# Attention's scores and value products in plain fp32: no halves, and the value products at two places of 64 columns

## The chip, the cores and the metric

The kernel runs on one core of a Trainium2 chip. The metric is the device time of one execution in microseconds (us); the median of three executions is given. Engines are named as in the profile: PE is TensorE (PEld its weight loads), DVE is VectorE, ACT is ScalarE, POOL is GpSimd, SP is SyncE, which here only issues DMAs.

## The reference

One layer of a hybrid decoder for 1024 prompt tokens and 8 single-token samples. The part that the change touches is the prompt's attention, 8 heads, causal:

```python
s = (jnp.einsum('bqhd,bkhd->bhqk', qn_b, k_nope, preferred_element_type=jnp.float32)
     + jnp.einsum('bqhr,bkr->bhqk', qr_b, krope, preferred_element_type=jnp.float32)) * scale
s = jnp.where(kpos[None, :] <= qpos[:, None], s, -jnp.inf)
p = jax.nn.softmax(s, axis=-1)
return jnp.einsum('bhqk,bkhd->bqhd', p.astype(v.dtype), v)
```

A key has 64 + 32 = 96 features, a value 64. Around it stand two feed-forward blocks of width 2816, an input projection, an mLSTM group, the samples' attention over 64 pages, an output projection, and a per-layer embedding. All data are fp32.

## The kernel before

Activations lie transposed, features on partitions, 1032 tokens (1024 + 8) along the free axis, in three groups of 344. Every large product is computed from halves: an fp32 operand x is split into `hi` (x rounded to the type fp32r, an ACT cast) and `lo` (x - hi, a DVE or POOL subtraction; the helper `split`), and a product is three fp32r matmuls, hi·hi + hi·lo + lo·hi (`mm3`, lines 196 to 198). Small products, such as those of the mLSTM chunks, the norms' sums and the samples' attention, are plain fp32 matmuls; each of these is two instructions on PE in the trace.

The order of PE's and SP's instructions is that in which the code emits them; the tile framework orders DVE, ACT and POOL. The `Emitter` puts slow chains (samples' attention, per-layer embedding projection) step by step between units of tensor work. Large tiles come from one pool of 43 buffers (`big`, helper `B`) that are reused in the order in which they come free.

Prompt attention, as it stands:

- The projections make q, k and v. `q_rope`, `q_nope` and `k_pair` split their results and write both halves to DRAM; `load_head` reads a head's q and k back, 6 DMAs for a head. `v_all` keeps v in SBUF, for each of 8 key blocks a tile of 8 heads x (64 columns of hi, 64 of lo).
- `att_s` takes query blocks of 128 in two halves Q = 0, 1 of a head. For each it makes the scores (up to 512 keys a matmul group, three matmuls of 128 to 512 columns, tile `pss`), the masked maximum (DVE), the exponential with its sum (ACT), the reciprocal and the normalisation (DVE or ACT). Result: P.
- `att_pv` takes the four query blocks of a half together. For each key block kb it transposes the live blocks of P on PE (`pT`), and evacuates them as halves: ACT casts hi, then DVE subtracts lo (tile `PT`). Then two matmuls of up to 512 columns accumulate into `po`, with the stationary operand [v hi | v lo] of 128 columns, so that rows 0 to 63 of `po` collect v hi's part and rows 64 to 127 v lo's. At the end ACT copies one part and DVE adds the other (`aT`).

Transposes run `SKEW` = 3 key blocks ahead of the products, scores 3 blocks of queries ahead (`LEAD`). A head's two halves give 12 key-block steps, 96 steps in all; 48 of them have all four query blocks live (512 columns), 16 each have 3, 2 and 1 (384, 256, 128 columns).

The samples' attention (`sample_attention`, lines 1026 to 1140) runs among this: POOL gathers pages by indirect DMA (`kt`, `nt`, 128 gathers), and PE multiplies them at four places of 32 columns each (`ss`, line 1072; `ol`, line 1118), in plain fp32.

Of the kernel before, what the change touches and what calls it, by code (L numbers as in the profile page):

```python
# [7 lines left out]
F32 = mybir.dt.float32  # L8
F32R = mybir.dt.float32r
# [44 lines left out]
ACT_NORM = (1, 3, 5)  # L54
SKEW = 3
LEAD = 3
AHEAD = 4
# [33 lines left out]
class Emitter:  # L91
    """Orders what is emitted: a step can be put off until some microseconds of tensor work lie before it,
    and slow chains are taken step by step between the units of tensor work."""

# [37 lines left out]
def trunk(ctx: ExitStack, tc, I, O):  # L132
# [73 lines left out]
    class Acts:  # L206
        """Eight feature tiles, split, cut by token group: 15 of a group's 16 slices in five tiles of its own."""

# [74 lines left out]
    class Norm:  # L283
# [137 lines left out]

    # ---- start
    ones = C([128, 128], name="ones")
# [50 lines left out]

    # ---- constants of the mixing part
    ident = C([128, 128], name="ident")
# [28 lines left out]

    # ---- input projection
    zs = {}
# [66 lines left out]
    def gates():  # L574
# [90 lines left out]

    # ---- mLSTM of the prompt, a chunk a step
    xd = tc.dram_tile([MH, 128, NC, CH], F32, name="xd")
# [87 lines left out]

    # ---- norms of the latents
    cks = C([128, 2, NB_S], name="cks")
# [14 lines left out]

    # ---- one step of the mLSTM for the samples, a head at a time
    xs = C([128, MH * NB_S], name="xs")
# [87 lines left out]

    # ---- MLA projections, kept in DRAM until their head's turn
    vd = tc.dram_tile([8, 128, HEADS * 128], F32, name="vtd")
    kd = tc.dram_tile([HEADS * 64, 2, S], F32, name="ktd")
    qnd = tc.dram_tile([HEADS * 64, 2, T], F32, name="qnd")
    qrd = tc.dram_tile([HEADS * 32, 2, T], F32, name="qrd")
    qz = qzr[0:96, :].rearrange("p (a b c) -> p a b c", a=3, b=NB_S)
# [20 lines left out]
    def put_q(dst, rows, qp):  # L889
        def f():  # L890
            for i in range(2):
                sp.dma_start(out=dst[rows, i, :], in_=qp[i].bitcast(F32))
        em.later(6.0, f)

    def q_rope(r, w):
        qp = pair("qr")
        for g in range(G):
            c = GS[g]
            p1, p2 = PS([128, N]), PS([128, N])
            mmk(p1, w[0], cq, c)  # L900
            mmk(p2, w[1], cq, c)
            qf, t2 = SC(p="qf"), SC(p="t2")
            dve.tensor_tensor(out=qf, in0=p1, in1=cos4[:, c], op=ALU.mult)
            dve.tensor_tensor(out=t2, in0=p2, in1=sin4[:, c], op=ALU.mult)
            pool.tensor_tensor(out=qf, in0=qf, in1=t2, op=ALU.add)
            split(qp[0][:, c], qp[1][:, c], qf, pool)
            if g == G - 1:
                for j in range(4):
                    dve.tensor_copy(qz[64:96, 2, :, 4 * r + j], qf[32 * j:32 * j + 32, N - NB_S:N])
            em.spend(2.6)  # L910
        put_q(qrd, slice(128 * r, 128 * r + 128), qp)

    def q_nope(p, w):
        ukT = B([64, 2, 256], F32, "ukT")
        sp.dma_start(out=ukT, in_=I["w_ukT"][:, 2 * p:2 * p + 2, :])
        qp = pair("qn")
        for g in range(G):
            c = GS[g]
            ps = PS([128, N])
            mmk(ps, w, cq, c)  # L920
            split(qp[0][:, c], qp[1][:, c], ps)
            if g == G - 1:
# [31 lines left out]
    def k_pair(p, w):  # L954
        for hf in range(2):
            c = slice(hf * 512, (hf + 1) * 512)
            ps = PS([128, 512])
            mmk(ps, (w[0][:, p], w[1][:, p]), ck, c)
            kk = B([128, 2, 512], F32R, "kk")
            split(kk[:, 0], kk[:, 1], ps)  # L960
            em.later(KD_LAT, lambda c=c, kk=kk: sp.dma_start(out=kd[128 * p:128 * p + 128, :, c], in_=kk.bitcast(F32)))
            em.spend(1.3)

    def v_all(uvh, uvl):
        for kb in range(8):
            ps = PS([128, 512])
            t = slice(kb * 128, (kb + 1) * 128)
            for ct in range(2):
                mm3(ps, ck[ct][0][:, t], ck[ct][1][:, t], uvh[:, ct, :], uvl[:, ct, :], ct == 0, ct == 1)
            vv = B([128, HEADS, 128], F32R, "vv")  # L970
            split(vv[:, :, 0:64], vv[:, :, 64:128], ps.rearrange("p (h v) -> p h v", h=HEADS))
            vtok.append(vv)
            em.spend(1.3)
            yield

    def load_head(hd):
        kp = kT[hd % 2]
        qp = (B([96, S], F32R, "qTh"), B([96, S], F32R, "qTl"))
        for i in range(2):
            sp.dma_start(out=qp[i][0:64, :].bitcast(F32), in_=qnd[64 * hd:64 * hd + 64, i, 0:S])  # L980
            sp.dma_start(out=qp[i][64:96, :].bitcast(F32), in_=qrd[32 * hd:32 * hd + 32, i, 0:S])
            sp.dma_start(out=kp[i][0:64, :].bitcast(F32), in_=kd[64 * hd:64 * hd + 64, i, :])
        return qp
# [15 lines left out]
    for p in range(4):  # L999
        k_pair(p, uk)  # L1000
        if p == KT_AT:
            kT = []
            for i in range(2):
                kp = (B([128, S], F32R, "kTh"), B([128, S], F32R, "kTl"))
                split(kp[0][64:96, :], kp[1][64:96, :], kr[:, 0:S], pool)
                kT.append(kp)
            kr = None
        if p == LH_AT:
            qps = {0: load_head(0)}
# [5 lines left out]

    # ---- attention of the samples over their pages
    NI = NB_S * N_PAGES
# [122 lines left out]

    # ---- attention of the prompt
    em.flush()

    def att_s(hd, qp, Q, P):
        kp = kT[hd % 2]
        for qb in range(4 * Q, 4 * Q + 4):
# [13 lines left out]
            for kg in range(nkg):  # L1160
                n = min(512, nk - 512 * kg)
                ps = PS([128, 512], "pss")
                kc = slice(512 * kg, 512 * kg + n)
                pe.matmul(ps[:, 0:n], qp[0][:, qs], kp[0][0:96, kc], start=True, stop=False)
                pe.matmul(ps[:, 0:n], qp[0][:, qs], kp[1][0:96, kc], start=False, stop=False)
                pe.matmul(ps[:, 0:n], qp[1][:, qs], kp[0][0:96, kc], start=False, stop=True)
                if kg == nkg - 1:
# [19 lines left out]
    def att_pv(hd, P, Q):  # L1187
        po = PS([128, 512], "po")
        nkb = 4 * Q + 4
        pxs = {}  # L1190

        def tr(kb):
            j0 = max(0, kb - 4 * Q)
            ps = PS([128, 4, 128], "pT")
            for j in range(j0, 4):
                pe.transpose(ps[:, j, :], P[j][:, kb * 128:(kb + 1) * 128], ident)
            px = B([128, 2, 4, 128], F32R, "PT")
            split(px[:, 0, j0:4, :], px[:, 1, j0:4, :], ps[:, j0:4, :])
            pxs[kb] = px
# [4 lines left out]
        for kb in range(nkb):  # L1204
# [4 lines left out]
            px = pxs.pop(kb)  # L1209
            for i in range(2):  # L1210
                pe.matmul(po[:, j0 * 128:512], vtok[kb][:, hd, :], px[:, i, j0:4, :].rearrange("p j q -> p (j q)"),  # L1211
                          start=(kb == 0 and i == 0), stop=(kb == nkb - 1 and i == 1))
            px = None
        r0 = 64 * (hd % 2)
        t = aT[hd // 2][r0:r0 + 64, 512 * Q:512 * Q + 512]
        act.copy(t, po[0:64])
        dve.tensor_tensor(out=t, in0=po[64:128], in1=t, op=ALU.add)
        yield
# [56 lines left out]

    # ---- output projection of the mixing part
    n2 = Norm(None, "xn", G_FF2)
# [142 lines left out]

    # ---- per-layer embedding and the final norm
    def ple_unit(m, g):
# [168 lines left out]
```

## Time and profile before

| what | value |
|---|---|
| three executions | 2379.78, 2379.93, 2381.81 us; median 2379.93 |
| span of the profiled execution | 2381.1 us (clock granted on average 0.980) |
| PE busy | 2294.8 us, 96% of the span |
| DVE, ACT, POOL busy | 1084.0, 732.8, 416.5 us |
| chain that ended last | PE 82%, DVE 9%, DMA 4%, ACT 3% |

The profiled execution's time is given by its span alone; it lies between the lowest and the highest of the three, 1.2 us over the median. "Busy" of PE includes the end of each matmul that overlaps the next one's start, so that a busy PE need not be at its peak. Prompt attention lies from 1144 us (first `pss`) to about 1419 us (last `po`) after the start.

### The profile page before, as it was taken

The page shows a single profiled execution, that of the slowest core. Times are in us where ns is not written, and L with a number is a line of the kernel's source. Part 1 is how long each engine was busy: PE and PEld are TensorE (multiplying, and loading weights), DVE is VectorE, ACT ScalarE, POOL GpSimd, SP SyncE. Part 2 cuts the span into 40 slices and gives each one's busy share as a digit, 9 for nine tenths or more (in the row PEclk, how much of TensorE's full clock was granted, in tenths as well). Part 3 has the DMA queues.
Part 4 walks back from the last instruction along what each step waited for, and adds up shares of the span by engine and source line. Part 5 has one row for each costly group of instructions (what it writes and reads, how often), then busy time and mean ns, then how long its engine had stood idle before and what let it go on. Part 6 is the DMA issues. An engine that isn't in the chain of part 4 may idle for free.

```text
span 2381.1 us, 35330 instructions
## 1 busy us (share of the span) xinstructions
PE 2294.8 (96%) x14479; PEld 2220.7 (93%) x14479; DVE 1084.0 (46%) x2231; ACT 732.8 (31%) x1496; POOL 416.5 (17%) x403
## 2 busy tenths in 40 slices
PE   8999999999998999999888889999999999999997
PEld 7999999999998999999666679999999999999996
DVE  7332332333335656447766677623223223223575
ACT  5211211202213334444655553411121120211353
POOL 4101101101103321102565314200000000000233
PEclk9999999999999999999989989999999999999998
DMA  3111011120121313224964530111111112112213
GB/s 134 38 52 60 29 55 54 32 75 28 43 75 59 109 48 93 82 86 165 260 164 134 160 136 28 45 38 52 55 33 54 56 32 70 33 38 78 62 38 107
DMA packets 77883, 177.84 MB, mean 75 GB/s; under 512 B 11200, under 2 KB 37408, under 8 KB 77720
## 3 DMA queue, kind: packets, MB, share of 16 engines
q1 hardware_dynamic: 67432, 153.22, 21.1%
q0 software_dynamic: 6832, 18.12, 2.9%
q10 hardware_dynamic: 3456, 4.23, 0.6%
q8 instruction: 114, 1.87, 0.3%
q14 instruction: 49, 0.40, 0.1%
HBM read 146.58 MB, written 28.95 MB: 74 GB/s over the span
## 4 chain that ended last, share of the span: by engine, by line
PE 82%; DVE 9%; DMA 4%; ACT 3%; issue 2%; POOL 1%; SPq 0%; ACTq 0%; DVEq 0%; POOLq 0%
PE pd L197 7%; PE pd L198 7%; PE pd L196 7%; PE pg L198 7%; PE pu L197 7%; PE pu L196 7%; PE pu L198 7%; PE pg L197 7%; PE pg L196 7%; PE pz L197 3%; PE pz L196 3%; PE pz L198 3%; DVE xf L279 2%; PE po L1211 1%; DMA kt<-in_cT,idx_t 1%
## 5 line engine op out<-in xcount | busy, mean ns | idle before, releaser
L196 PE MATMUL pd<-hdh,wh 128*128 128x344 f32 x1056 | 341.0, 323 | 5.8 <-ACT hdh L178 5.8
L197 PE MATMUL pd<-hdl,wh 128*128 128x344 f32 x1056 | 340.0, 322 | 3.4 <-DVE hdl L182 3.3
L197 PE MATMUL pg<-xn,wh 128*128 128x344 f32 x1056 | 338.6, 321 | 4.5 <-DVE xn L182 3.8
L198 PE MATMUL pd<-hdh,wl 128*128 128x344 f32 x1056 | 339.7, 322 | 0.0
L196 PE MATMUL pg<-xn,wh 128*128 128x344 f32 x1056 | 338.1, 320 | 0.9 <-ACT xn L178 0.9
L196 PE MATMUL pu<-xn,wh 128*128 128x344 f32 x1056 | 338.5, 321 | 0.3 <-DVE si L347 0.3
L198 PE MATMUL pu<-xn,wl 128*128 128x344 f32 x1056 | 337.8, 320 | 0.8 <-DVE wl L182 0.8
L198 PE MATMUL pg<-xn,wl 128*128 128x344 f32 x1056 | 337.9, 320 | 0.5 <-DVE wl L182 0.3
L197 PE MATMUL pu<-xn,wh 128*128 128x344 f32 x1056 | 337.9, 320 | 0.0
L178 ACT CAST wh<-wr 128x1024 fp32r<-128x1024 f32 (+2 forms) x195 | 180.4, 935 | 371.8 <-PE pd L197 291.2
L182 DVE TENSOR_TENSOR wl<-wr,wh 128x1024 fp32r<-128x1024 f32 (+2 forms) x195 | 215.5, 1105 | 116.3 <-ACT wh L178 111.5
L353 DVE TENSOR_TENSOR hp<-si,pu 128x344 f32<-128x344 f32 x132 | 67.7, 513 | 420.5 <-PE pu L198 413.0
L365 DVE SCALAR_TENSOR_TENSOR h<-pd,h 128x344 f32<-128x344 f32 x240 | 123.2, 515 | 280.1 <-PE pd L198 280.1
L254 POOL TENSOR_TENSOR sq<-sq,sq 128x344 f32<-128x344 f32 x66 | 70.6, 1070 | 798.6 <-ACT sq L249 770.7
L196 PEld LDWEIGHTS pd<-hdh,wh 128*128 128x128 f32 x1056 | 200.0, 189 | 7.1 <-ACT hdh L178 6.7
L197 PEld LDWEIGHTS pg<-xn,wh 128*128 128x128 f32 x1056 | 198.7, 188 | 6.4 <-DVE xn L182 5.2
L197 PEld LDWEIGHTS pd<-hdl,wh 128*128 128x128 f32 x1056 | 200.0, 189 | 4.6 <-DVE hdl L182 4.2
L198 PEld LDWEIGHTS pd<-hdh,wl 128*128 128x128 f32 x1056 | 200.0, 189 | 0.0
L196 PEld LDWEIGHTS pg<-xn,wh 128*128 128x128 f32 x1056 | 198.6, 188 | 1.5 <-ACT xn L178 1.2
L198 PEld LDWEIGHTS pg<-xn,wl 128*128 128x128 f32 x1056 | 198.7, 188 | 1.1 <-DVE wl L182 1.1
L198 PEld LDWEIGHTS pu<-xn,wl 128*128 128x128 f32 x1056 | 198.6, 188 | 1.1 <-DVE wl L182 1.1
L196 PEld LDWEIGHTS pu<-xn,wh 128*128 128x128 f32 x1056 | 198.6, 188 | 1.0 <-issue 0.8
(384 smaller groups left out, 4174.9 us busy)
## 6 DMA issues: line engine op xcount, KB each, us to landing
wr<-in_wu SPq DMA_DIRECT2D x44, 512.0 KB, 3.6
wr<-in_wg SPq DMA_DIRECT2D x43, 512.0 KB, 3.7
wr<-in_wd SPq DMA_DIRECT2D x64, 320.0 KB, 2.9
wr<-in_w_in SPq DMA_DIRECT2D x22, 512.0 KB, 3.8
h<-in_xT SPq DMA_DIRECT2D x24, 172.0 KB, 4.2
hsp<-h SPq DMA_DIRECT2D x8, 516.0 KB, 3.4
ppd<-pj SPq DMA_DIRECT2D x24, 172.0 KB, 2.2
h<-hsp SPq DMA_DIRECT2D x8, 516.0 KB, 5.9
```

Of the source, the lines that this page charges most:

```text
L178: act.copy(hi, src)
L182: dve.tensor_tensor(out=lo, in0=src, in1=hi.bitcast(F32), op=ALU.subtract)
L196: pe.matmul(ps, whi, xhi, start=first, stop=False)
L197: pe.matmul(ps, whi, xlo, start=False, stop=False)
L198: pe.matmul(ps, wlo, xhi, start=False, stop=last)
L254: pool.tensor_tensor(out=acc[0], in0=acc[0], in1=q, op=ALU.add)
L279: dve.scalar_tensor_tensor(out=x, in0=s[:, c], scalar=gc[:, g0 + k:g0 + k + 1], in1=r, op0=ALU.mult, op1=ALU.mult)
L353: dve.tensor_tensor(out=p, in0=s, in1=pu, op=ALU.mult)
L365: dve.scalar_tensor_tensor(out=h[m][:, c], in0=pd, scalar=0.5, in1=h[m][:, c], op0=ALU.mult, op1=ALU.add)
L1211: pe.matmul(po[:, j0 * 128:512], vtok[kb][:, hd, :], px[:, i, j0:4, :].rearrange("p j q -> p (j q)"), start=(kb == 0 and i == 0), stop=(kb ...
```

## The change

Scores and value products take fp32 operands as they are. No q, k, v or P is split. A score group is one fp32 matmul instead of three of halves. v is kept as 64 columns a head. In `att_pv` a key block's four transposed query blocks stand in the order 0, 3, 1, 2 (`PV_POS`); the first two are multiplied at columns 0 to 63 of the array, the other two at columns 64 to 127, 256 columns each, with the same v. `PV_LIVE` says which are live on the diagonal. `po` is 256 columns wide, its lower 64 rows holding query blocks 0 and 3, its upper 64 rows 1 and 2. One copy evacuates a transposed block, by DVE for even and by ACT for odd key blocks, and two key blocks share a tile `PT`. Two ACT copies take `po` to `aT`. `load_head` issues 3 DMAs instead of 6; the projections write one DMA where there were two, and `k_pair` one for both halves of the keys.

```diff
     def k_pair(p, w):
-            kk = B([128, 2, 512], F32R, "kk")
-            split(kk[:, 0], kk[:, 1], ps)
-            em.later(KD_LAT, lambda c=c, kk=kk: sp.dma_start(out=kd[128 * p:128 * p + 128, :, c], in_=kk.bitcast(F32)))
+            if hf == 0:
+                kk = B([128, S], F32, "kk")
+            act.copy(kk[:, c], ps)
+            if hf == 1:
+                em.later(KD_LAT, lambda: sp.dma_start(out=kd[128 * p:128 * p + 128, :], in_=kk))
...
     def load_head(hd):
-        qp = (B([96, S], F32R, "qTh"), B([96, S], F32R, "qTl"))
-        for i in range(2):
-            sp.dma_start(out=qp[i][0:64, :].bitcast(F32), in_=qnd[64 * hd:64 * hd + 64, i, 0:S])
-            sp.dma_start(out=qp[i][64:96, :].bitcast(F32), in_=qrd[32 * hd:32 * hd + 32, i, 0:S])
-            sp.dma_start(out=kp[i][0:64, :].bitcast(F32), in_=kd[64 * hd:64 * hd + 64, i, :])
+        qp = B([96, S], F32, "qT")
+        sp.dma_start(out=qp[0:64, :], in_=qnd[64 * hd:64 * hd + 64, :])
+        sp.dma_start(out=kp[0:64, :], in_=kd[64 * hd:64 * hd + 64, :])
+        sp.dma_start(out=qp[64:96, :], in_=qrd[32 * hd:32 * hd + 32, :])
...
     def att_s(hd, qp, Q, P):
-                pe.matmul(ps[:, 0:n], qp[0][:, qs], kp[0][0:96, kc], start=True, stop=False)
-                pe.matmul(ps[:, 0:n], qp[0][:, qs], kp[1][0:96, kc], start=False, stop=False)
-                pe.matmul(ps[:, 0:n], qp[1][:, qs], kp[0][0:96, kc], start=False, stop=True)
+                pe.matmul(ps[:, 0:n], qp[:, qs], kp[0:96, kc], start=True, stop=True)
...
     def att_pv(hd, P, Q):
-        po = PS([128, 512], "po")
+        po = PS([128, 256], "po")
...
-                pe.transpose(ps[:, j, :], P[j][:, kb * 128:(kb + 1) * 128], ident)
-            px = B([128, 2, 4, 128], F32R, "PT")
-            split(px[:, 0, j0:4, :], px[:, 1, j0:4, :], ps[:, j0:4, :])
+                pe.transpose(ps[:, PV_POS[j], :], P[j][:, kb * 128:(kb + 1) * 128], ident)
+            if kb % 2 == 0:
+                pts[:] = [B([128, 2, 4, 128], F32, "PT")]
+            px = pts[0][:, kb % 2]
+            live = (slice(0, 4), slice(1, 4), slice(1, 4, 2), slice(1, 2))[j0]
+            if kb % 2 == 0:
+                dve.tensor_copy(px[:, live, :], ps[:, live, :])
+            else:
+                act.copy(px[:, live, :], ps[:, live, :])
...
-            for i in range(2):
-                pe.matmul(po[:, j0 * 128:512], vtok[kb][:, hd, :], px[:, i, j0:4, :].rearrange("p j q -> p (j q)"),
-                          start=(kb == 0 and i == 0), stop=(kb == nkb - 1 and i == 1))
+            v = vtok[kb][:, 64 * hd:64 * hd + 64]
+            for i, p0 in enumerate(PV_LIVE[j0]):
+                if p0 < 2:
+                    pe.matmul(po[64 * i:64 * i + 64, p0 * 128:256], v, px[:, 2 * i + p0:2 * i + 2, :].rearrange("p j q -> p (j q)"),
+                              start=kb == 0, stop=kb == nkb - 1 - i)
```

`q_rope`, `q_nope` and `v_all` lose their `split` in the same way (one ACT or DVE copy, or none).

On PE, where the second half of head 0 is multiplied with v (`pss` scores of a later block, `ss` the samples' pages, `pT` transposes of P, `po` the value products), there stood before:

```order
L1164 MATMUL pss_11144<-kTh_10529,qTh_10754 128x512
L1165 MATMUL pss_11144<-kTl_10530,qTh_10754 128x512
L1166 MATMUL pss_11144<-kTh_10529,qTl_10755 128x512
L1164 MATMUL pss_11149<-kTh_10529,qTh_10754 128x256
L1165 MATMUL pss_11149<-kTl_10530,qTh_10754 128x256
L1166 MATMUL pss_11149<-kTh_10529,qTl_10755 128x256
L1211 MATMUL po_10989<-PT_11057,vv_10696 128x512 x2
L1196 MATMUL pT_11163<-ident,P_10876 128x128
L1211 MATMUL po_10989<-PT_11095,vv_10729 128x512 x2
L1211 MATMUL po_10989<-PT_11104,vv_10751 128x384 x2
```

and now, at the same place:

```order
L1166 MATMUL pss_11005<-kT_10479,qT_10671 128x512
L1166 MATMUL pss_11008<-kT_10479,qT_10671 128x256
L1221 MATMUL po_10870<-PT_10925,vv_10603 64x256 x2
L1198 MATMUL pT_11020<-ident,P_10773 128x128
L1221 MATMUL po_10870<-PT_10960,vv_10651 64x256 x2
L1221 MATMUL po_10870<-PT_10960,vv_10651 64x128
L1221 MATMUL po_10870<-PT_10960,vv_10651 64x256
```

Nothing has moved past anything else on PE: the same steps follow each other, with fewer and different matmuls in them. Over the kernel the value products stand in 75 unbroken runs, before as now, with transposes, scores or other products of the full array between them.

On SP, where head 1 is loaded (`qnd`, `qrd`, `ktd` are the DRAM copies of q's two parts and of k; `nk` belongs to the samples, `out_n_s` is an output), there stood before:

```order
L980 DMA qTh_10754<-qnd 64x1024
L981 DMA qTh_10754<-qrd 32x1024
L982 DMA kTh_10529<-ktd 64x1024
L980 DMA qTl_10755<-qnd 64x1024
L981 DMA qTl_10755<-qrd 32x1024
L982 DMA kTl_10530<-ktd 64x1024
L1030 DMA nk<-cks 96x8
```

and now:

```order
L814 DMA out_n_s<-nst 128x32
L982 DMA qT_10671<-qnd 64x1024
L983 DMA kT_10479<-ktd 64x1024
L984 DMA qT_10671<-qrd 32x1024
L1032 DMA nk<-cks 96x8
```

Three transfers of a head's six are gone, for each of the 8 heads; SP's whole queue is 34 transfers shorter.

## Rows read from the trace of the kernel before

**Rows 1.** The page's 40 slices of the span, 59.5 us each, in tenths:

```profile
PE   8999999999998999999888889999999999999997
PEclk9999999999999999999989989999999999999998
```

**Rows 2.** Busy time by stretch: length, engines' busy us (instructions), granted clock, DMA share, GB/s:

```profile
1060.00:1144.00 84.00, 80.08 (x498) 74.61 (x497) 58.50 (x173) 42.65 (x98) 22.38 (x17) 0.96 0.55 182
...
1165.00:1200.00 35.00, 30.94 (x186) 20.21 (x186) 19.65 (x60) 18.35 (x48) 26.46 (x28) 0.76 0.83 212
1200.00:1250.00 50.00, 40.94 (x280) 31.59 (x279) 35.42 (x105) 29.14 (x79) 31.81 (x34) 0.91 0.64 169
1250.00:1300.00 50.00, 45.77 (x306) 35.40 (x304) 34.61 (x112) 30.74 (x86) 22.66 (x25) 0.98 0.46 128
1300.00:1350.00 50.00, 41.02 (x267) 31.78 (x268) 28.80 (x86) 25.52 (x68) 29.37 (x32) 0.84 0.60 161
1350.00:1419.00 69.00, 57.58 (x340) 49.05 (x339) 53.72 (x136) 46.31 (x112) 8.20 (x7) 0.90 0.42 147
```

**Rows 3.** Waits of PE, 1140 to 1420 us: total us, times, longest:

```profile
PE ss L1072 <- DMA kt<-in_cT,idx_t: 7.0, 7, 2.8
PE ol L1118 <- DMA nt<-in_cN,idx_n: 6.3, 3, 2.5
PE po L1211 <- DVE PT L182: 6.1, 11, 1.1
PE pT L1196 <- DVE PT L182: 5.9, 1, 5.9
```

**Rows 4.** Timeline of PE, fp32r scores of 512 and of 128 columns:

```profile
1229.83 0.39 PE L1165 MATMUL pss<-kTl,qTh 96*128 96x512 f32 x1
1230.06 0.40 PE L1166 MATMUL pss<-kTh,qTl 96*128 96x512 f32 x1
...
1230.90 0.28 PE L1165 MATMUL pss<-kTl,qTh 96*128 96x128 f32 x1
1231.02 0.28 PE L1166 MATMUL pss<-kTh,qTl 96*128 96x128 f32 x1
```

**Rows 5.** Timeline of PE, plain fp32 products on the full array, two instructions each:

```profile
979.81 0.39 PE L708 MATMUL pc<-vt,kw 128*128 128x129 f32 x2
980.04 0.39 PE L711 MATMUL pab<-vt,w 128*128 128x129 f32 x2
...
2289.17 0.74 PE L263 MATMUL ns<-sq,ones 128*128 128x344 f32 x2
...
2289.91 0.32 PE L197 MATMUL pl<-xp,wh 128*128 128x344 f32 x1
2290.07 0.32 PE L198 MATMUL pl<-xp,wl 128*128 128x344 f32 x1
```

**Rows 6.** Timeline of PE around a samples' block at four places of 32 columns:

```profile
1274.17 0.60 PE L1196 MATMUL pT<-ident,P 128*128 128x128 f32 x4
1274.70 1.50 PE L1072 MATMUL ss<-kt,qz 96*32 96x256 f32 x24
1276.13 0.50 PE L1164 MATMUL pss<-kTh,qTh 96*128 96x512 f32 x1
1276.46 0.39 PE L1165 MATMUL pss<-kTl,qTh 96*128 96x512 f32 x1
```

**Rows 7.** Groups by line: evacuations; busy us, mean ns, idle before:

```profile
L182 DVE TENSOR_TENSOR PT<-pT,PT 128x512 fp32r<-128x512 f32 (+1 forms) x96 | 50.3, 549 | 6.2 <-ACT PT L178 5.6
L178 ACT CAST PT<-pT 128x512 fp32r<-128x512 f32 (+1 forms) x96 | 43.3, 489 | 12.4 <-PE pT L1196 12.2
L1217 DVE TENSOR_TENSOR aT<-po,aT 64x512 f32<-64x512 f32 x16 | 11.1, 694 | 1.0 <-ACT aT L1216 0.2
L544 DVE COPY z<-pz 128x344 f32<-128x344 f32 x15 | 7.3, 496 | 4.5 <-PE pz L198 4.5
```

**Rows 8.** Waits of POOL, 1140 to 1420 us: total us, times, longest:

```profile
POOL nt L1058 <- PE po L1211: 17.7, 5, 9.0
```

More of the change, by code (lines that the diff above doesn't have):

```diff
@@ L55 @@
 SKEW = 3
+PV_POS = (0, 2, 3, 1)
+PV_LIVE = ((0, 0), (1, 0), (1, 1), (1, 2))
 LEAD = 3
@@ L864, in trunk @@
     vd = tc.dram_tile([8, 128, HEADS * 128], F32, name="vtd")
-    kd = tc.dram_tile([HEADS * 64, 2, S], F32, name="ktd")
-    qnd = tc.dram_tile([HEADS * 64, 2, T], F32, name="qnd")
-    qrd = tc.dram_tile([HEADS * 32, 2, T], F32, name="qrd")
+    kd = tc.dram_tile([HEADS * 64, S], F32, name="ktd")
+    qnd = tc.dram_tile([HEADS * 64, S], F32, name="qnd")
+    qrd = tc.dram_tile([HEADS * 32, S], F32, name="qrd")
     qz = qzr[0:96, :].rearrange("p (a b c) -> p a b c", a=3, b=NB_S)
@@ L890, in f @@
         def f():
-            for i in range(2):
-                sp.dma_start(out=dst[rows, i, :], in_=qp[i].bitcast(F32))
+            sp.dma_start(out=dst[rows, :], in_=qp[:, 0:S])
         em.later(6.0, f)
     def q_rope(r, w):
-        qp = pair("qr")
+        qp = B([128, T], F32, "qr")
         for g in range(G):
@@ L901, in q_rope @@
             mmk(p2, w[1], cq, c)
-            qf, t2 = SC(p="qf"), SC(p="t2")
+            qf, t2 = qp[:, c], SC(p="t2")
             dve.tensor_tensor(out=qf, in0=p1, in1=cos4[:, c], op=ALU.mult)
@@ L905, in q_rope @@
             pool.tensor_tensor(out=qf, in0=qf, in1=t2, op=ALU.add)
-            split(qp[0][:, c], qp[1][:, c], qf, pool)
             if g == G - 1:
@@ L915, in q_nope @@
         sp.dma_start(out=ukT, in_=I["w_ukT"][:, 2 * p:2 * p + 2, :])
-        qp = pair("qn")
+        qp = B([128, T], F32, "qn")
         for g in range(G):
@@ L920, in q_nope @@
             mmk(ps, w, cq, c)
-            split(qp[0][:, c], qp[1][:, c], ps)
+            act.copy(qp[:, c], ps)
             if g == G - 1:
@@ L969, in v_all @@
                 mm3(ps, ck[ct][0][:, t], ck[ct][1][:, t], uvh[:, ct, :], uvl[:, ct, :], ct == 0, ct == 1)
-            vv = B([128, HEADS, 128], F32R, "vv")
-            split(vv[:, :, 0:64], vv[:, :, 64:128], ps.rearrange("p (h v) -> p h v", h=HEADS))
-            vtok.append(vv)
+            if kb % 2 == 0:
+                vv = B([128, 2, HEADS * 64], F32, "vv")
+            dve.tensor_copy(vv[:, kb % 2], ps)
+            vtok.append(vv[:, kb % 2])
             em.spend(1.3)
@@ L1003, in trunk @@
             for i in range(2):
-                kp = (B([128, S], F32R, "kTh"), B([128, S], F32R, "kTl"))
-                split(kp[0][64:96, :], kp[1][64:96, :], kr[:, 0:S], pool)
+                kp = B([128, S], F32, "kT")
+                pool.tensor_copy(kp[64:96, :], kr[:, 0:S])
                 kT.append(kp)
@@ L1187, in att_pv @@
     def att_pv(hd, P, Q):
-        po = PS([128, 512], "po")
+        po = PS([128, 256], "po")
         nkb = 4 * Q + 4
         pxs = {}
+        pts = []
         def tr(kb):
@@ L1195, in tr @@
             for j in range(j0, 4):
-                pe.transpose(ps[:, j, :], P[j][:, kb * 128:(kb + 1) * 128], ident)
-            px = B([128, 2, 4, 128], F32R, "PT")
-            split(px[:, 0, j0:4, :], px[:, 1, j0:4, :], ps[:, j0:4, :])
+                pe.transpose(ps[:, PV_POS[j], :], P[j][:, kb * 128:(kb + 1) * 128], ident)
[3 more added lines that the diff above has]
+            live = (slice(0, 4), slice(1, 4), slice(1, 4, 2), slice(1, 2))[j0]
+            if kb % 2 == 0:
+                dve.tensor_copy(px[:, live, :], ps[:, live, :])
+            else:
+                act.copy(px[:, live, :], ps[:, live, :])
             pxs[kb] = px
@@ L1209, in att_pv @@
             px = pxs.pop(kb)
-            for i in range(2):
-                pe.matmul(po[:, j0 * 128:512], vtok[kb][:, hd, :], px[:, i, j0:4, :].rearrange("p j q -> p (j q)"),
-                          start=(kb == 0 and i == 0), stop=(kb == nkb - 1 and i == 1))
+            v = vtok[kb][:, 64 * hd:64 * hd + 64]
[3 more added lines that the diff above has]
+                              start=kb == 0, stop=kb == nkb - 1 - i)
             px = None
         r0 = 64 * (hd % 2)
-        t = aT[hd // 2][r0:r0 + 64, 512 * Q:512 * Q + 512]
-        act.copy(t, po[0:64])
-        dve.tensor_tensor(out=t, in0=po[64:128], in1=t, op=ALU.add)
+        t = aT[hd // 2][r0:r0 + 64, 512 * Q:512 * Q + 512].rearrange("p (j q) -> p j q", j=4)
+        act.copy(t[:, 0:4:3, :], po[0:64].rearrange("p (j q) -> p j q", j=2))
+        act.copy(t[:, 1:3, :], po[64:128].rearrange("p (j q) -> p j q", j=2))
+        pts.clear()
         yield
```

## The prediction

> **What bounds the kernel now.** I read the slices first. PE stands at 9 tenths nearly everywhere, and at 8 in five slices in a row, the twentieth to the twenty-fourth, which are 1131 to 1428 us, the stretch of attention; in two of them the granted clock shows 8 tenths as well [rows 1]. The stage before, where q, k and v are made, has PE busy 80.08 of 84 us [rows 2]: whatever DVE and ACT lose there by no longer splitting hides behind PE and is worth at most those 4 idle us, 1 by my choice. So the change is decided between 1144 and 1419 us.
>
> In that stretch no single engine is the bound. Between 1165 and 1419 us PE is idle 4.1 + 9.1 + 4.2 + 9.0 + 11.4 = 38 us, while DVE is busy 54 to 78% of each window [rows 2]. The clock is granted at 0.76 to 0.98 of full speed; as it knows only 1.2 and 2.4 GHz, a mean c over a window means (1 - c)/0.5 of it at the lower one: 16.8 + 9 + 2 + 16 + 13.8 = 58 us [rows 2]. Work done there takes twice as long, so this costs up to 29 us; PE is idle for part of it, and I take 24. What PE waits for is of two kinds: the samples' gathered pages, 7.0 + 6.3 us, and the evacuation of transposed P, 6.1 + 5.9 us [rows 3]. The clock is lowest in the two windows that hold gathers (0.76 and 0.84) and nearly full in 1250 to 1300, which has few [rows 2].
>
> **Scores: +10 us.** A 512-column fp32r matmul takes 0.23 us from start to start, 0.455 ns a column; one of 128 columns 0.12 [rows 4]. Three of them: 0.70 us at 512, 0.525 at 384, 0.35 at 256, 0.35 at 128. Plain fp32 is two instructions: 0.23 us for 129 columns; and a pair of 344 columns, with one fp32r matmul of 0.16 behind it, takes 0.74, so 0.58 alone [rows 5]. Both give 1.7 ns a column: 0.87 us at 512, 0.65 at 384, 0.435 at 256, 0.22 at 128. There are 48 score groups of 512 and 16 of each other size: 48 x 0.17 + 16 x (0.125 + 0.085 - 0.13) = 8.2 + 1.3, some 10 us of PE work more. DVE and ACT wait 0.17 us longer for a full group.
>
> **Value products: 0 if the two places run side by side.** A full step was two fp32r matmuls of 512 columns, 0.47 us. It becomes two fp32 matmuls of 256 columns, 0.435 us each. No row shows two places of 64. The nearest is the samples' block at four places of 32: 24 instructions of 256 columns, 12 matmuls, in 1.43 us [rows 6], where one after another 12 x 0.435 = 5.2 us would be needed; four abreast 1.31. So I take side by side: 48 full steps save 1.5 us; the 16 steps with three live blocks (0.435 for 0.35) give 1.4 back, the others change by nothing. The other bound is one after another: 48 x 0.40 + 16 x (0.305 + 0.20) = +27 us.
>
> The Trainium skill's "TensorE: Matmul & The Clock Gate" (Part 3) measured only 2.38x for three matmuls side by side in columns. By that share of the ideal two places would give 1.59x, a full step 0.55 us and the value products +6 us in all; the samples' block shows the fuller overlap, 3.6x of 4, drains included.
>
> **Changes of the array's shape: +20 us.** This is the price that the diff does not show. Before the samples' block the fourth transpose starts at about 1274.50 (three steps of 0.11 from 1274.17) and should be done at 1274.61; the block starts at 1274.70, 0.09 late. It takes 0.12 over 1.31. The score matmul behind it takes 0.33 to the next start, where 0.23 is usual: 0.10 [rows 4, 6]. In all 0.31 us for going into the split array and out again. Value products stand in 75 runs with full-array work on both sides, so 75 x 0.31 = 23 us; with 64 columns to load in place of 32, perhaps 25. Some runs wait for their `PT` anyway (11 waits in [rows 3]) and drain meanwhile: I take 20. Bounds: 10, if PE's idle time swallows half of it, and 25.
>
> "TensorEngine Tiling (Array Packing)" in the Trainium skill says under Key Properties that changing the tiling mode drains the engine. This is the rule that speaks against the change; it gives no price, and without it the sum would be 20 us lower.
>
> **Evacuation: -9 us.** DVE loses 96 subtractions (50.3 us) and 16 additions (11.1). It gets 48 copies; one of 344 columns takes 0.50 us [rows 7], so with 512 about 0.67 and over the mix of sizes about 0.55: 26 us. DVE does 35 us less. ACT loses 96 casts of 0.49 (43.3 us) for 48 copies like them, 23 us, and has 32 copies to `aT` where it had 16. The chain from a transpose to its product is one operation of 0.5 to 0.7 us where it was two [rows 7]. PE's 12 us of waits for `PT` [rows 3] should fall to about 4, and waits for softmax by 1.
>
> **Gathers: -11 us.** Tiles of P, q, k and v go from two halves to one: 8 tiles of v become 4, a head's q and k 2 instead of 4, `PT` one for two steps. The 43 buffers are reused in the order of release, so each gather gets a buffer that has been free for longer; POOL waited 17.7 us for PE to release them [rows 8]. SP's queue has 34 transfers fewer ahead of the page table and the loads. I let PE's 13.3 us of waits for pages [rows 3] fall to 3, and add 1 for k's first load. If POOL's own pace sets the pages' arrival, this gain is 4; then PE is held up later by the same pages.
>
> **Clock: -11 us.** Where those stalls go, part of the 58 us at 1.2 GHz should go: I take 11 of the 24 us that they cost. Bounds: 0, and 18.
>
> **The rest: -5 us.** 30 us of new PE work stretch the stage for DVE, ACT and POOL, which have less to do. Of the 38 - 13 - 12 = 13 idle us that are left, I let 5 be filled. With 1 for the projections the sum is 10 + 0 + 20 - 9 - 11 - 11 - 5 - 1 = -7 us.
>
> The sum is against the profiled execution, whose span of 2381.1 us is 1.2 over the median, so the median should move from 2379.9 to 2373. 0.2% of it, 4.8 us, is about what a measurement here can tell from no change.
>
> **Rivals.**
> - *The gains and the prices cancel.* For it: +30 of new PE work is counted from rows, -37 is waits and clock, counted by choice. If the clock follows only half as well (-5) the sum is -1. Time 2376 to 2384. Chance 0.20.
> - *The shape changes make PE the bound: slower.* The 75 drains stand in PE's own queue, and nothing behind them can start. If all are paid (25 us), and POOL's pace keeps the pages late (gain 4) and with them the clock (-5), the sum is 10 + 25 - 9 - 4 - 5 - 5 - 1 = +11 us: 2391. It decides as soon as gathers and clock together give back less than 10. For it: POOL is busy 26.46 of 35 us where the first gathers run [rows 2]. Against it: POOL's wait for buffers [rows 8] is longer than PE's wait for pages. Chance 0.18.
> - *The two places do not run side by side*, so the change does not do what it says: +27 on PE, of which the remaining idle time takes 5 or so, -7 + 22: 2395, up to 2402 with full drains. Against it: the four places [rows 6]. Chance 0.10.
> - *By the 1.59x of above* the time would be 2379, inside the first rival; the trace bears it out so poorly that it adds nothing to its chance.
>
> **How the numbers follow.** The forecast has a chance of 0.52, with its own range from 2353 (clock -18, half of the drains hidden, gathers all gone) to 2375. Faster by over 0.2%: 0.52; within: 0.20; slower: 0.18 + 0.10 = 0.28. The range takes in the first two rivals and most of the third: 2352 to 2401.
>
> **What would show it.** `pss` of 512 columns: two instructions, 0.87 us from the first to the next work. `po`: instructions at both places starting within some hundredths of a us; if the second starts 0.4 us after the first, the third rival is right. Runs of `po` followed by a late first weight load, about 0.3 us a run. PE's waits for `PT` under 5 us, for `kt` and `nt` together under 5, and a granted clock over 0.92 in 1165 to 1419. The forecast is wrong if the clock stays at 0.9 or below although the page waits are gone, if the split array is itself given a lower clock, or if a run costs clearly more than 0.31 us.

## The result, and the profile after

The changed kernel takes 2342.53 us (median of 4 runs, 2340.30 to 2347.29) beside 2379.86 for the kernel before on the same chip: ratio 0.9843, 95% interval 0.9829 to 0.9858, or 37 us less. The forecast was 2373 us, with a range from 2352 to 2401; the time lies below it. The direction was right, the size was not.

The 40 slices of the changed kernel's page, to be read beside [rows 1]; the five slices with an 8 and the two with a low clock are gone:

```profile
PE   8999999999999899999999999999999999999997
PEclk9999999999999999999999999999999999999998
```

Its windows over the same kind of stretches as [rows 2] (length, busy us of PE, PEld, DVE, ACT and POOL with their instructions, granted clock, DMA share, GB/s):

```profile
1060.00:1139.00 79.00, 77.26 (x505) 72.69 (x504) 51.54 (x165) 39.64 (x92) 14.56 (x11) 1.00 0.45 148
1139.00:1200.00 61.00, 56.06 (x349) 33.80 (x348) 42.62 (x146) 35.25 (x93) 45.82 (x49) 0.94 0.72 188
1200.00:1260.00 60.00, 60.00 (x404) 37.08 (x404) 36.85 (x120) 35.48 (x99) 38.40 (x41) 1.00 0.57 158
1260.00:1320.00 60.00, 60.00 (x441) 34.99 (x438) 38.46 (x121) 35.66 (x101) 39.06 (x40) 1.00 0.53 143
1320.00:1380.00 60.00, 56.11 (x348) 37.51 (x345) 42.56 (x109) 39.53 (x94) 7.92 (x7) 0.94 0.53 179
```

From 1200 to 1320 us PE has no idle time at all and the full clock. What it still waits for, 1135 to 1425 us (total us, times, longest), beside [rows 3]: pages 1.9 us where they were 13.3, `PT` 2.4 + 1.5 where it was 12.0:

```profile
PE pT L1198 <- ACT PT L1206: 2.4, 1, 2.4
PE ss L1074 <- DMA kt<-in_cT,idx_t: 1.9, 1, 1.9
PE wom L200 <- DVE wl L184: 1.7, 1, 1.7
PE pj L198 <- ACT wj L180: 1.6, 1, 1.6
PE pj L200 <- DVE wj L184: 1.5, 1, 1.5
PE po L1221 <- DVE PT L1204: 1.5, 1, 1.5
```

The new operations in PE's timeline: score groups of 512 columns, value products of one step (x4: two places, two instructions each) between single transposes, and of two steps (x8):

```profile
1208.89 0.65 PE L1221 MATMUL po<-PT,vv 128*64 128x256 f32 x4
1209.47 0.33 PE L1198 MATMUL pT<-ident,P 128*128 128x128 f32 x1
1209.73 0.65 PE L1221 MATMUL po<-PT,vv 128*64 128x256 f32 x4
...
1216.76 1.88 PE L1166 MATMUL pss<-kT,qT 96*128 96x512 f32 x4
1218.47 0.71 PE L1198 MATMUL pT<-ident,P 128*128 128x128 f32 x5
...
1265.39 1.08 PE L1221 MATMUL po<-PT,vv 128*64 128x256 f32 x8
1266.40 1.77 PE L1166 MATMUL pss<-kT,qT 96*128 96x512 f32 x4
```

Two score groups take 1.71 us from start to start, 0.855 each. One step of value products takes 0.58 to the next start, two take 1.01, so a step is worth 0.43: the two places run side by side. From one run (value products with no other matmul between them) to the next with one transpose between is 0.84 us, where 0.43 + 0.11 would do without a change of shape: 0.30 for out and in.

To see where the 37 us are, one window over the whole attention stage, from the first `pss` to the first `woa`, is best. First the kernel before, then the changed one:

```profile
1144.60:1412.60 268.00, 227.72 (x1419) 175.68 (x1418) 183.11 (x557) 161.86 (x416) 128.03 (x133) 0.89 0.59 162
```

```profile
1139.40:1372.20 232.80, 223.97 (x1484) 135.62 (x1483) 155.44 (x484) 140.72 (x375) 129.59 (x133) 0.97 0.59 167
```

The stage is 35.2 us shorter and starts 5.2 us earlier. I split its length into PE's idle time, what the lower clock costs (as in the prediction: (1 - c)/0.5 of the window, half of it, times PE's busy share) and the rest, PE's work at full clock. Before: 40.3 idle, 0.11/0.5 x 268 = 59 us at 1.2 GHz costing 59/2 x 0.85 = 25, work 202.6. After: 8.8 idle, 14 us at 1.2 GHz costing 6.7, work 217.3. So idle -31.5, clock -18.4, work +14.7.

What the +14.7 is made of can be counted in the traces: the time from the start of one PE instruction to the start of the next, idle time left out and stretches at 1.2 GHz halved. Scores, transposes and value products together take 129.9 us before and 147.1 after, +17.2, with all changes of shape in it. The samples' blocks (`ss`, `ol`) take 27.7 before and 22.1 after, -5.6, though their instructions are the same. What else stands in the stage adds 3.

The two profiled executions are further apart than the medians: their spans are 2381.1 and 2338.5 us, 42.6 apart, beside 37.3. In all other runs the time of an execution is 1.7 to 2.1 us over its span; by that, an estimate, the profiled execution of the kernel before took some 2383 us, 3 over its median and not the 1.2 that the prediction took, and that of the changed kernel, 2340.3, lies 2.2 under its own. Some 5 us of the split are scatter of this kind.

### The profile page after: what moved, and what is told of

Read it like the earlier page. It is cut to its first block, busy times and chain, and to the rows that moved or that the text cites. A ratio compares the mean times of both kernels' runs of the same rounds, so it can differ in the third digit from the quotient of the medians.

```text
span 2338.5 us, 35223 instructions
## 1 busy us (share of the span) xinstructions
PE 2288.4 (98%) x14543; PEld 2178.7 (93%) x14543; DVE 1046.3 (45%) x2147; ACT 708.7 (30%) x1448; POOL 410.4 (18%) x397
## 4 chain that ended last, share of the span: by engine, by line
PE 89%; DVE 6%; ACT 2%; DMA 1%; issue 1%; POOL 0%; SPq 0%; DVEq 0%; ACTq 0%; POOLq 0%
PE pd L199 7%; PE pd L200 7%; PE pd L198 7%; PE pg L200 7%; PE pu L199 7%; PE pu L198 7%; PE pu L200 7%; PE pg L199 7%; PE pg L198 7%; PE pz L199 3%; PE pz L198 3%; PE pz L200 3%; PE pss L1166 3%; DVE xf L281 2%; PE po L1221 2%; PE pT L1198 2%
## 5 line engine op out<-in xcount | busy, mean ns | idle before, releaser
L198 PEld LDWEIGHTS pu<-xn,wh 128*128 128x128 f32 x1056 | 199.0, 188 | 1.0 <-issue 0.8
L199 PEld LDWEIGHTS pu<-xn,wh 128*128 128x128 f32 x1056 | 199.0, 188 | 0.2
```

What stands on the lines that cost most here:

```text
L198: pe.matmul(ps, whi, xhi, start=first, stop=False)
L199: pe.matmul(ps, whi, xlo, start=False, stop=False)
```

## The experiments

Chips are numbered in the order of the experiments. On the first and the fifth the kernel before takes 2378 and 2380 us, as it does beside the result above, on the second to fourth 2422, 2427 and 2427 (last section), so times are compared with neighbours on one chip. On the first and the fifth chip the changed kernel was not run beside the others; its 2342.5 us from the result stands in for it, and the kernels before there lie within 1.5 us of the one beside that result. On the fourth it was not run either. Theory A: room, that is tiles and loads freed, brings the pages in time. Theory B: the shorter evacuation of transposed P. Theory C: longer PE work is taken by idle time.

**Scores alone, value products alone (first chip).**

```
e1: + q, k, att_s of the changed kernel;  v_all, att_pv as before
e2: + v_all, att_pv of the changed kernel;  q, k, att_s as before
```

> Only q, k and the scores go to plain fp32; v, transposed P and the value products stay split as before. Theory A (room: tiles released earlier let the samples' gathers start earlier): 4 of the some 10 big tiles in hand during attention are freed and a head's loads halve, against 10 us more of score work on PE: 2360 to 2375 us, page waits well under the 13 us of before, waits for PT as before (12 us). Theory B (the shorter evacuation of transposed P and the relief of DVE carry the gain): nothing of that is in here, so 2380 to 2390 us, the scores' price alone. Theory C (slower scores give DVE and ACT time, so that the longer PE work itself fills the idle time): 2365 to 2380, with PE's idle time down by 10 and page waits as before.

> Only v, transposed P and the value products go to plain fp32 at two places; q, k and the scores stay split. Theory A: 6 of the some 10 tiles are freed, the shape changes cost their 20 us: 2360 to 2372 us, page waits down to under 5 us. Theory B: the whole gain and none of the scores' price: 2330 to 2342 us, waits for PT near 0 while page waits may stay. Theory C: 2375 to 2395, the shape changes without the cover of slower scores.

Measured: 2354.8 and 2363.5 beside 2378.4 us, ratios 0.9898 (0.9881 to 0.9914) and 0.9936 (0.9920 to 0.9953): -24 and -15 us, which add up to the whole, 37, or a little more. B is out as the sole cause, since the scores alone gain most, and more than A said. C's ranges miss both. With the scores alone the waits for pages are 4.7 us, and the first gather begins at 1139.6 us. The value products alone still wait 10.1 us for `kt` pages, twice what A allowed, though the time lies in A's range; there the first gather begins at 1150.5 us, as late as in the kernel before.

**Room taken back (first chip).** Of each tile one half is used; `kT` and `PT` are treated likewise.

```
-            if kb % 2 == 0:
-                vv = B([128, 2, HEADS * 64], F32, "vv")
+            vv = B([128, 2, HEADS * 64], F32, "vv")
...
-        qp = B([96, S], F32, "qT")
+        qp = (B([96, S], F32, "qT"), B([96, S], F32, "qT"))
```

> The changed kernel with its freed room taken back: each tile of v, of PT, of q and of k is allocated as often as before and filled only half, and q and k are loaded in as many transfers as before, with half the bytes. Nothing that PE, DVE or ACT compute changes. Theory A (room): gathers wait for buffers as before, the page waits (13 us) and most of the clock loss come back: 2362 to 2378 us. Theory B (evacuation chain and DVE's load): unchanged, 2340 to 2348 us.

Measured: 2358.7, 16 us over the changed kernel's 2342.5: far from B, short of A's range. The edit takes back tiles and transfers at once, so it doesn't part the two. Page waits come back in part (5.3 + 2.4 us), and POOL waits for PE to release buffers again. Its timeline of gathers: the first `kt`, and the first `nt` after a wait, of the kernel before,

```profile
1151.23 1.01 POOL L1049 DMA_INDIRECT kt<-in_cT,idx_t  x1 [10.83 <-PE ps L198]
...
1209.06 0.94 POOL L1058 DMA_INDIRECT nt<-in_cN,idx_n  x1 [7.73 <-PE po L1211]
...
1349.98 0.94 POOL L1058 DMA_INDIRECT nt<-in_cN,idx_n  x1 [0.30 <-issue]
```

of the changed kernel (first `kt`, first and last `nt`),

```profile
1139.55 1.02 POOL L1051 DMA_INDIRECT kt<-in_cT,idx_t  x1 [28.86 <-DVE dn L822]
...
1179.30 0.97 POOL L1060 DMA_INDIRECT nt<-in_cN,idx_n  x1 [0.30 <-ACT aT L1227]
...
1310.01 0.95 POOL L1060 DMA_INDIRECT nt<-in_cN,idx_n  x1 [0.30 <-issue]
```

and of the half-filled one:

```profile
1140.62 1.02 POOL L1053 DMA_INDIRECT kt<-in_cT,idx_t  x1 [29.72 <-DVE vv L973]
...
1183.81 0.98 POOL L1062 DMA_INDIRECT nt<-in_cN,idx_n  x1 [3.89 <-PE po L1221]
...
1334.28 0.95 POOL L1062 DMA_INDIRECT nt<-in_cN,idx_n  x1 [0.30 <-issue]
```

The changed kernel's gathers begin 11.7 us earlier and end 40 us earlier; with half-filled tiles they begin early and end late.

**The two-operation chain (first chip).**

```
-                dve.tensor_copy(px[:, live, :], ps[:, live, :])
-            else:
-                act.copy(px[:, live, :], ps[:, live, :])
+            act.copy(px[:, live, :], ps[:, live, :])
+            dve.tensor_tensor(out=px[:, live, :], in0=ps[:, live, :], in1=px[:, live, :], op=ALU.max)
```

> The changed kernel with the evacuation of transposed P made two operations again: ACT copies every tile, then DVE takes the maximum of the PSUM tile and the copy, which is the same value; 96 operations on each of the two engines, as before. Tiles in hand and PE's work are those of the changed kernel. Theory A (room): waits for PT come back by some 6 to 10 us, pages stay in time: 2345 to 2354 us. Theory B: DVE is again 60 to 75% busy, the chain is long, stalls and clock loss come back: 2360 to 2378 us.

Measured: 2348.7, 6 us more, in A's range; the runs lie between 2346.6 and 2357.4, and the 95% interval of the ratio (0.9854 to 0.9889) leaves 1 to 9 us. In the profiled execution, the slowest of the four, waits for `PT` are 7.6 us where the changed kernel had 3.9, less than A said, and pages stay in time (1.6).

**Room and chain together (second, third, fourth chip).** Both edits in one kernel.

> Both undone in the changed kernel: half-filled tiles with as many loads as before, and the two-operation evacuation. Alone they cost 16 and 6 us. If the prediction's 30 us of new PE work is really paid, and was outweighed by room and chain, then both together must cost far more than 22 us, since only the lighter projections are left as a gain: 2385 to 2405 us. If the new PE work is mostly not paid, because stalls that took as long are gone with it, the two add up: 2360 to 2370 us.

> The changed kernel itself once more, as the neighbour of the three below: on the chip of their first runs the kernel before took 2422 us, 42 more than elsewhere, and the changed kernel was not among them. If this is a chip like the first: 2340 to 2346 us. If it is like the second: the changed kernel has the gathers' slowness too, 2375 to 2400 us against 2422.

> Half-filled tiles and the two-operation evacuation together, beside the changed kernel: 43 to 60 us more than it if the 30 us of new PE work was paid and outweighed; 20 to 28 us more if the two prices (16 and 6) simply add up.

> Room and chain both taken back. Where the kernel before takes 2380 us: 2385 to 2405 us if the 30 us of new PE work is paid once the two reliefs are gone, 2360 to 2368 us if the prices of 16 and 6 us add up. Where the kernel before takes over 2415 us: 2420 to 2432.

Measured: 2423.2, 2429.4 and 2428.9 us, ratios to the kernel before 1.0009, 1.0009 and 1.0012 (the last 1.0003 to 1.0022). The changed kernel itself on the third chip: 2409.0, ratio 0.9930 (0.9914 to 0.9947), above what I had allowed it. So with both reliefs gone the time is that of the kernel before, although the slower scores and all shape changes are still in. On the third chip that is 20 us over the changed kernel, near the sum of the two prices that the first chip gave (16 + 6), and not 43. The third expectation's range for such a chip, 2420 to 2432, can't tell the two cases apart. In these profiles PE is idle for 54 to 59 us of the stage, so new PE work may well be cheaper there than elsewhere; on a chip like the first, where the gain is 37 us, the two edits were not run together, and some 15 us of the gain belong to neither price.

**One place; the full array (second, third, fourth chip).**

```
one place:  po[0:64, j0 * 128:512] <- v of 64 columns, px[:, j0:4]        (fp32, 512 columns)
full array: po[:, j0 * 128:512]    <- v of two heads, 128 columns, px[:, j0:4]
```

> The changed kernel with the value products at one place of 64 columns alone: one fp32 matmul of 512 columns a step in place of two of 256 side by side. Shape changes, tiles and evacuation stay. By the sum of the prediction PE gets 48 x 0.435 + 16 x 0.3 or so = 24 to 27 us more: 2366 to 2370 us, since the changed kernel has under 9 us of idle PE time in attention to take it. Rival (the two places were not worth their time, something else sets the pace): under 2352 us.

> The changed kernel with the value products on the full array: the stationary side is 128 columns, v of two heads, of which 64 rows of the output are used, and one fp32 matmul of 512 columns a step; no change of the array's shape is left around them. Against the one-place kernel only the shape changes differ. If a round trip costs what the prediction took (20 us in all, bounds 10 and 25): 10 to 25 us under the one-place kernel, 2345 to 2358 us. Rival (the shape changes hide behind waits or cost little net): within 7 us of the one-place kernel.

> The value products at one place again, now beside the changed kernel: by the count of matmuls 24 to 27 us more than its neighbour. Rival (PE's length does not set the pace): under 10 us more.

> The full array again, beside the changed kernel and the one place: 10 to 25 us less than the one place if the shape changes cost what the prediction took, within 7 us of it if their net price is small. On the second chip it was 4 us less, between two times that both hung on late pages.

> One place of 64 columns again. On a chip where the kernel before takes 2380 us: 2358 to 2370 us, 16 to 27 over the changed kernel (16 is what it was on the third chip). Where the kernel before takes over 2415 us: 2415 to 2426.

> The full array again. Where the kernel before takes 2380 us: 10 to 25 us under the one place if shape changes cost what the prediction took; the third chip showed 12 and the second 4. Where the kernel before takes over 2415 us: 2409 to 2415.

Measured: one place 2416.2, 2424.7, 2426.0; full array 2411.9, 2412.8, 2411.8. On the third chip one place costs 16 us more than two (24 to 27 were counted), and the full array is 12 us below one place, 14 on the fourth, 4 on the second, for 75 runs of shape changes. These times alone don't settle the prices, as these chips stall in this stage, but PE's work in the traces does, counted as above. One place has 24.4 us more of it than the changed kernel (244.6 and 220.2, third chip): the price of not going side by side is all there, and a part is taken by idle time and by a higher clock. The full array has 18.7, 17.1 and 16.5 us less than one place (second to fourth chip): this is what the changes of shape cost on PE, as far as nothing but the shape (and the width of the stationary side, 64 or 128 columns) differs. The same place of the program on one place of 64 columns, then on the full array, 1.48 us from run to run and 1.18:

```profile
1252.15 1.07 PE L1219 MATMUL po<-PT,vv 128*64 128x512 f32 x2
1253.15 0.55 PE L1198 MATMUL pT<-ident,P 128*128 128x128 f32 x3
1253.63 1.07 PE L1219 MATMUL po<-PT,vv 128*64 128x512 f32 x2
```

```profile
1248.90 1.02 PE L1219 MATMUL po<-PT,vv 128*128 128x512 f32 x2
1249.76 0.49 PE L1198 MATMUL pT<-ident,P 128*128 128x128 f32 x3
1250.08 1.02 PE L1219 MATMUL po<-PT,vv 128*128 128x512 f32 x2
```

**Pages gathered once (before: second chip; changed: fourth).**

```
+            if "t" in once:
+                return once["t"]
-            out = []
+            out = once["t"] = []
```

> The kernel before, with the samples' pages gathered once and used for all of their products: PE, DVE and ACT do all their work, POOL and the DMA queues leave out the later gathers, and no gather needs a buffer later on. Output of the samples is not the reference's. If page waits and the clock that falls with them carry the gain (theory A): 2345 to 2360 us. If they carry only what the prediction gave them (11 us and a part of the clock): 2362 to 2371 us.

> The changed kernel with the samples' pages gathered once and used for all products (the samples' output is not the reference's). The kernel before, with its pages gathered once, took 2356 us. If late pages and the clock that falls with them were most of the gain, the two come out close: 2345 to 2356 us. If the shorter chain, the smaller load of DVE and ACT and the longer PE work behind them carry most: 2322 to 2338 us.

Measured: 2356.4 (2351.6 to 2356.9) and 2349.5 (2345.1 to 2350.9). Their attention stages, before and changed:

```profile
1145.00:1389.20 244.20, 212.79 (x1419) 169.69 (x1419) 181.42 (x558) 161.58 (x416) 17.92 (x17) 0.92 0.40 110
```

```profile
1140.70:1375.30 234.60, 224.95 (x1484) 136.23 (x1483) 153.77 (x484) 140.56 (x375) 18.12 (x17) 0.96 0.33 96
```

Without later gathers the kernel before is 23.8 us shorter in this stage than with them (268.0), the changed kernel not at all (232.8 with them). Both comparisons are between chips, as the stages with all gathers are those of the result's profiles. The samples' blocks fall from 27.7 to 21.1 us in the kernel before when its pages are all there, so late pages also cost PE work, as this count has it. In the kernel before, a block is done in pieces when it waits in its middle:

```profile
1239.48 1.06 PE L1118 MATMUL ol<-nt,spT 128*32 128x256 f32 x12
1242.59 0.62 PE L1118 MATMUL ol<-nt,spT 128*32 128x256 f32 x2 [2.06 <-DMA nt<-in_cN,idx_n]
1245.75 1.06 PE L1118 MATMUL ol<-nt,spT 128*32 128x256 f32 x2 [2.54 <-DMA nt<-in_cN,idx_n]
```

Between the two kernels 9.6 us are left: idle 31.4 to 9.7, clock 17 to 9, work +20. Both times fall in the ranges given for late pages: these are the larger part of the gain, not all of it.

**A fixed amount of PE work on either kernel (fifth chip).**

```
before:   +                for again in range(2):
          +                    pe.matmul(ps[:, 0:n], qp[0][:, qs], kp[0][0:96, kc], start=True, stop=True)
changed:  +                for again in range(qb % 2):
          +                    pe.matmul(ps[:, 0:n], qp[:, qs], kp[0:96, kc], start=True, stop=True)
```

> The kernel before with two more matmuls ahead of each score group (the same product, overwritten by the next): 2 x 17.6 = 35 us more work on PE and nothing else. If new PE work in the attention stage is paid, as the prediction's sum had it for its 30 us: 25 to 35 us over the kernel before. If it is mostly taken by idle time, because PE arrives later at waits that end at the same moment: under 18 us.

> The changed kernel with every second row block's score matmul done twice: 8 x (2 x 0.435 + 4 x 0.87) less the small ones = 35 us more work on PE. Its PE has under 9 us of idle time in this stage on the chip of its first profile, so it should pay 26 to 35 us there (2368 to 2378 us, or 0.994 of the kernel before); on chips where the kernel before takes over 2415 us, where it waits more, 10 to 30 over its 2409.

Measured: 2384.1 beside 2379.9 for the kernel before, ratio 1.0020 (1.0009 to 1.0030), so 35 us more of PE work cost 4 (2 to 7 by the interval). On the changed kernel: 2371.5, 29 over its 2342.5 (the fifth chip's kernel before is within 0.1 us of the one beside the result). The stages, before and changed with the extra work:

```profile
1143.30:1415.40 272.10, 247.23 (x1612) 198.81 (x1611) 186.10 (x558) 162.37 (x416) 130.03 (x133) 0.94 0.58 161
```

```profile
1139.40:1402.00 262.60, 256.70 (x1577) 153.05 (x1576) 159.91 (x483) 141.02 (x375) 128.97 (x133) 0.97 0.52 147
```

In the kernel before the extra work shows as 29.7 us at full clock: the score matmuls take 34.4 us longer, PE's other work 4.6 less. Idle falls from 40.3 to 24.9, and the lower clock, 0.89 before and 0.94 now, costs 14.9 us where it cost 25. Together +4.1. Of PE's waits named in [rows 3], the 13.3 us for pages fall to 7.8 and the 12.0 for `PT` to 9.7:

```profile
PE pT L1198 <- DVE PT L182: 6.0, 1, 6.0
PE ss L1072 <- DMA kt<-in_cT,idx_t: 5.6, 4, 2.3
PE po L1213 <- DVE PT L182: 3.7, 4, 1.5
PE ol L1118 <- DMA nt<-in_cN,idx_n: 2.2, 2, 1.4
```

The changed kernel has 8.8 us of idle time to give, gives 3, and pays the rest.

## Why the direction was right and the size wrong

The sum had idle -25 (evacuation 9, gathers 11, rest 5), clock -11 and new work +30 in the stage; the windows show -31.5, -18.4 and +14.7. All three err to the same side. The signs that the prediction named all came out: 0.855 us for a score group, two places side by side, 0.30 us for a run, waits for `PT` and for pages under 5 us each, a clock over 0.92. They checked the terms one by one, and none of them checked how the terms add up.

- **Scores: right.** 0.855 us a full group for the 0.87 taken.
- **Side by side: right.** 0.43 us a step; the row that decided it, four places of 32 in [rows 6], carried over. The Trainium skill's "TensorE: Matmul & The Clock Gate" (Part 3) measured 2.38x for three matmuls side by side in columns; the 0.55 us a step that the prediction estimated from it does not hold here.
- **Changes of shape, +20: right for PE, wrong as a difference.** A run costs 0.30 us (0.31 predicted), and full array against one place shows 16.5 to 18.7 us of PE work. "TensorEngine Tiling (Array Packing)" in the Trainium skill states under Key Properties that changing the tiling mode drains the engine; the trace agrees with these 0.30 us. (Of the 150 edges of the 75 runs, 12 border on the samples' blocks, which split the array before as now; the prediction put full-array work on both sides of all.) But the kernel before was not free of such losses: by the prediction's own prices its scores, transposes and value products should take 53 + 32 + 36 = 121 us of PE, and they take 129.9; the changed kernel's should take 63 + 32 + 35, some 129, and take 147.1. So some 9 us more are lost now, by this estimate, and not 20. Where the kernel before lost its 9 was not traced.
- **Gathers and clock, -22 together: right in kind.** Leaving the gathers out of the kernel before gives 23.8 us (on another chip), but in three parts: idle, clock, and 6.6 us of PE work in the samples' blocks, which the sum had at nothing; in the change itself these blocks give 5.6. POOL's own pace was not the limit: the same 1.2 us a gather, begun 11.7 us earlier, of which 5.2 are the stage's own earlier start. That early begin comes with the edit to q, k and the scores (1139.6 us with it alone, 1150.5 with the value products alone). That it is SP's shorter queue ahead of the page table was only argued: it also holds with as many q and k loads in the half-filled kernel.
- **Evacuation: -9, and 6 measured** (1 to 9) when the chain is made two operations again. PE's waits for `PT` fell to 3.9 us, as foreseen (4).
- **The rest, -5: the step that failed.** "30 us of new PE work stretch the stage for DVE, ACT and POOL ... I let 5 be filled." So the sum let the time grow by 25 for the new work. The profile shows 14.7 of new work, and of the idle time that is neither of pages nor of `PT` 12 us filled: 31.5 less 11.4 for pages and 8.1 for `PT`. The fixed-work run tests the step alone: of 35 us of new score work on the kernel before, 31 vanish, 15 in idle time, 10 in less time at the lower clock, and 5 because PE's other work gets shorter. I counted waits as a fixed stock from which each term took its share, and PE's work as paid on top. In that run 5.5 us of the waits for pages and 2.3 of those for `PT` go through added work alone. The two ways of filling share one stock, however: the 31 us can't be taken off the forecast on top of gathers, evacuation and clock, which claim the same idle time. Room and chain taken back points the same way (the kernel before's time, with the new PE work in), but in stages with 54 to 59 us of idle time.
- **Clock, as a part of this: -11, and 18 measured.** I tied it to the stalls that the other terms remove; in the fixed-work run it rises from 0.89 to 0.94 by added work alone.
- **Projections: -1, and the stage starts 5.2 us earlier.** Of these, some 3 us are clock again (0.96 before, 1.00 after in the window up to the first score), which the prediction didn't consider outside attention. Some 4 us come and go between executions: of 16 traces of kernels with the new q and k, the stage starts at 1138.7 to 1140.7 us in 11 and at 1142.9 to 1144.0 in five; with the old ones it starts at 1143.3 to 1145.0 in all four.

Between the two profiled executions the misses add up: 15 us less new work than forecast, 6.5 more idle time gone, 7.4 more of the clock's cost, 4 at the start of the stage and 2 behind it make 35, of which some 5 are scatter. How the 37 us of the medians divide among room, chain and filled idle time stays open: the terms share the same idle time, and room (16) and chain (6) were each measured on a kernel in which the other was in place.

## What to carry to other kernels

Where a stage has idle time on its busiest engine, price new work on it by what the waits behind it leave, not by its duration; a run that adds a fixed amount of dummy work to the kernel as it is tells this at once, and here gave 4 us for 35. The same work costs most of its price (29 of 35) after the waits are removed, so of two edits, one that adds work and one that takes waits away, the second to come finds another stage than the profile showed: don't sum both from the one profile, and don't book the same idle time twice. Price a new loss against what the same place loses already: here some 9 us were added where 20 were set down. Fewer buffers and loads for the same data (16 us) paid more than the operations saved (6): look at when the queue of gathers starts and ends, not only at the waits on it.

## What was not expected of the hardware

On three of five chips every kernel with all its gathers was slower, in the attention stage alone: the changed kernel's stage took 301 us on the third chip (first `pss` 1139.9, first `woa` 1440.9) and 232.8 beside the result, while the first `pss` came at 1139.9 and 1139.4 us and what follows the stage took 966.6 and 966.3. There engines stand still while the profile shows nothing that they wait for ("issue") or a releaser that it did not trace ("remote"); from the changed kernel's timeline on the third chip:

```profile
1156.12 0.69 DVE L974 COPY vv<-ps 128x512 f32<-128x512 f32 x1 [9.80 <-remote]
...
1156.87 0.79 PE L198 MATMUL ps<-uvh,ckh 128*128 128x512 f32 x1 [5.03 <-issue]
...
1162.88 0.69 ACT L1176 ACTIVATE P<-pss,nmx 128x512 f32<-128x512 f32 x1 [15.22 <-issue]
...
1172.96 0.69 DVE L974 COPY vv<-ps 128x512 f32<-128x512 f32 x1 [10.12 <-remote]
```

Without later gathers the kernel before took 2356 us on the second chip, the first of these three, 66 less than with them, so the gathers are part of it; why these chips differ was not found. The gain of the change is 18 us there (0.9930) instead of 37.
